# Rows of scores across four blocks in place of a carried state, in the gated linear recurrence of a hybrid block

## The chip, the cores and the metric

The kernel runs on one core of a Trainium2 chip. The metric is the device time of one execution in microseconds (us); of several runs the median counts, and lower is better. The core's engines work side by side, each through its own queue of instructions in order: TensorE (PE in the profile, with its weight loads as PEld), VectorE (DVE), ScalarE (ACT), GpSimd (POOL) and SyncE (SP), which issues most of the transfers (DMA).

## The reference, cut to what matters

One layer over 512 tokens of width 2048, all in float32. The input is normalised and projected; one branch is a gated linear recurrence (HGRN2) with 8 heads of 128 channels, the other a sparse attention in which an indexer scores all keys and the 128 best per query are kept. Both are gated, projected, merged, projected again and normalised. The recurrence is the part that changes most:

```python
def step(state, inp):            # one chunk of CHUNK = 64 tokens
    q_c, k_c, g_c, v_c = inp
    cum = jnp.cumsum(g_c, axis=1)                    # log of the decay
    inter = jnp.einsum('bthk,bhkv->bthv', q_c * jnp.exp(cum), state)
    diff = cum[:, :, None] - cum[:, None, :]
    decay = jnp.exp(jnp.where(causal[None, :, :, None, None], diff, -jnp.inf))
    scores = jnp.einsum('bthk,bshk,btshk->bhts', q_c, k_c, decay)
    intra = jnp.einsum('bhts,bshv->bthv', scores, v_c)
    last = cum[:, -1]
    new_state = (jnp.exp(last)[..., None] * state
                 + jnp.einsum('bshk,bshv->bhkv', k_c * jnp.exp(last[:, None] - cum), v_c))
    return new_state, inter + intra
...
top_val, top_idx = lax.top_k(score, topk)            # topk = 128, in the sparse branch
```

The chunk is only a way to compute it: the result is a causal sum over all earlier tokens, each with the product of the decays between the two tokens. So any grouping of the tokens gives the same output.

## The kernel before

The whole program is one list of jobs, and a job is a stretch of matmuls (projections of the normalised input, with weights that are loaded, split and multiplied chunk by chunk). The order is written out by hand: instructions are issued to each engine's queue in the order in which the Python code meets them. A large projection is done in three products of rounded parts (`mm3`, lines 75 to 77): `wh` is the rounded weight, `wl` what the rounding left, both made by `split` (line 71 on ScalarE, line 72 on VectorE) from the loaded `wr`. `prep(i, ahead)` issues the loads and splits of the chunks up to three ahead. `mm` (line 80) is a plain matmul.

Everything else runs in lanes: Python generators, each of which issues a small piece of work and yields. `pump()` is called every 24 matmuls or so of a job and lets each lane issue one piece: first the recurrence (`hgrn`), then the selection (`top`), then the attention (`att`), then norms and tables. So a piece of a lane stands in TensorE's queue between two runs of projection matmuls, and its results are needed when the next pump comes to the next piece.

The recurrence, `hgrn_gen(p)`, handles two heads at a time, in the order p = 3, 2, 0, 1, one pair after the other. Head `c` of a pair has four blocks of 128 tokens. Inside a block the scores are built in levels: level `l` multiplies queries of the second half of each group of 2^l tokens with keys of the first half (`scores`, small matmuls into `hl`), after which `decay(l)` (line 779, VectorE) multiplies those queries and keys with the running products `tot`. After level 7 a query carries the decay from its block's start, a key the decay to its block's end, and `S` holds the transposed score matrices inside the eight blocks of the pair (zeros are written by `G.memset` at level 4). Then come three pieces:

- the keys of the first three blocks are transposed on TensorE (`hkt`, line 852) and copied to `kd` (line 853, ScalarE);
- the states are built: `hp` holds keys times values for three blocks, line 865 copies the first into `st`, and line 867 adds the others with their decay, one after the other, on VectorE;
- the output `ho`: for each block the scores `S` times the values, and for all but the first the state `st` times the queries. ScalarE copies `ho` out, with its squares, and a norm and a gate follow.

All of these matmuls have plain float32 operands. The projections have operands of a rounded float32 type (fp32r in the profile's rows for the engines that write them).

The selection, `top_gen`, finds the 128 largest scores of each row in 16 rounds of MAX and MATCH_REPLACE on VectorE (lines 639 and 640), for widths of 256, 384 and 512 columns. It has a budget: at every pump it gets 2.7 less `R.load`, and a lane that puts much work on VectorE sets `R.load` high, so that fewer rounds are issued there.

At the start, `start()` reads the input in 16 parts, multiplies the first weights straight away (`pf`, line 80) and sums the squares of the input for the norm: `square(k)` on ScalarE, `add(k)` on VectorE (line 321). Five groups of parts are handled, and the squares of a group are taken one group later.

Of the kernel before, what the change touches and what calls it, by code (L numbers as in the profile page):

```python
# [50 lines left out]
def hybrid_block(ctx, tc, x, w_in, w_uq, w_qidx, w_ukv, w_pa, w_pb, w_out, rel_bias, final_norm_w,  # L51
# [207 lines left out]
    def start():  # L259
        R.v0 = enter("v0")  # L260
        R.x = enter("sums")
        p0 = enter("p0", side="right")
        R.xt = []
        for k in range(8):
            if k in (EVEN, EVEN + 1):
                R.x.tile([128, STILL if k == EVEN else 64 - STILL], F32, name=f"gap{k}")
            R.xt.append(R.x.tile([128, 2, T], F32, name=f"xt{k}", tag=f"sh{k}"))
            if k < 6:
                xs_l.append(R.x.tile([128, 4, 256], FR, name=f"sl{k}", tag=f"sl{k}"))
            else:  # L270
                R.dg = R.x.tile([128, 1024], F32, name=f"dg{k}", tag=f"sl{k}")
                if k == 6:
                    R.row, R.total = R.dg[:, 0:T], R.dg[:, T:]
        R.rinv = cols[:, 25:29]
        ident = R.dg[:, 0:128]
        parts = ((0, 2), (2, 4), (4, 8), (8, 12), (12, 16))
        wh, wl, wr = [], [], []
        sums = p0.tile([128, 2, T], F32, name="sums")

        def load_x(k, i=None):  # L280
            n = slice(0, 2) if i is None else slice(i, i + 1)
            SP.dma_start(R.xt[k][:, n, :], x_t[:, 2 * k + n.start:2 * k + n.stop, :])

        def load_w(c):
            k0, k1 = parts[c]
            wr.append(p0.tile([128, 4, 272], F32, name="fr", bufs=3))
            SP.dma_start(wr[c][:, 0:k1 - k0, :], w_first[:, k0:k1, :])

        A.dma_start(wc, w_norm)
        load_x(0, 0)  # L290
        load_w(0)
        load_x(0, 1)
        load_w(1)
        load_x(1)
        A.dma_start(ident, c_ident)
        A.dma_start(cols[:, 0:25], w_cols)

        def load_group(c):
            load_x(2 * c - 2)
            load_w(c)  # L300
            load_x(2 * c - 1)

        load_group(2)
        heat_src = p0.tile([128, 128], F32, name="rows")
        G.memset(heat_src, 1.0)
        G.tensor_copy(ones_r, heat_src)
        A.activation(R.rinv[:, 0:1], eps, AF.Sqrt)
        warm = mmp.tile([128, T], F32, name="acc")
        for _ in range(8):
            PE.matmul(warm[:, 0:128], ones, ones, start=True, stop=True)  # L310
        pools4 = [(mmp, "acc"), (sdp, "sd")] * 2
        accs = [pool.tile([128, T], F32, name="pf", tag=tag)[:, 0:272] for pool, tag in pools4]
        squares = {}

        def square(k):
            squares[k] = p0.tile([128, 2, T], F32, name="sq", bufs=3)
            A.activation(squares[k], R.xt[k], AF.Square)

        def add(k):
            if k:  # L320
                V.tensor_tensor(sums, squares.pop(0) if k == 1 else sums, squares.pop(k), op=OP.add)

        def three(c, n):
            k0, k1 = parts[c]
            xp, wp = ((xh, wh), (xl, wh), (xh, wl))[n]
            for k in range(k0, k1):
                for t in range(4):
                    mm(accs[t], xp[k // 4][:, k % 4, t * 128:t * 128 + 128], wp[c][:, k - k0, :],
                       k + n == 0, k == NK - 1 and n == 2)

        behind = ()
        for c, (k0, k1) in enumerate(parts):
            n = slice(0, k1 - k0)
            wh.append(p0.tile([128, 4, 272], FR, name="fh", bufs=3))
            wl.append(p0.tile([128, 4, 272], FR, name="fl", bufs=3))
            G.tensor_copy(wh[c][:, n], wr[c][:, n])
            for k in range(k0, k1):
                src = R.xt[k // 2][:, k % 2, :]
                hi, lo = xh[k // 4][:, k % 4, :], xl[k // 4][:, k % 4, :]
                A.activation(hi, src, AF.Copy, scale=wc[:, k:k + 1])  # L340
                V.scalar_tensor_tensor(lo, src, wc[:, k:k + 1], hi.bitcast(F32), op0=OP.mult, op1=OP.subtract)  # L341
            V.tensor_tensor(wl[c][:, n], wr[c][:, n], wh[c][:, n].bitcast(F32), op=OP.subtract)
            if c < 2:
                load_group(c + 3)
            if c == 2:
                load_ahead()
            if c == 4:
                prep(0, 1)
            pairs = range(k0 // 2, k1 // 2)
            for k in behind:  # L350
                square(k)
                add(k)
            behind = pairs
            for n in range(3):
                three(c, n)
        prep(0, 2)
        for k in behind:
            square(k)
            add(k)
        V.tensor_tensor(R.total, sums[:, 0, :], sums[:, 1, :], op=OP.add)  # L360
        R.first = accs
        leave("p0")
# [373 lines left out]
    def hgrn_gen(p):  # L736
        f, q = (hg[p, n] for n in "fq")
        gate = R.h.tile([128, 2, T], F32, name="hg")
        SP.dma_start(gate, gate_d[2 * p:2 * p + 2].rearrange("f p t -> p f t"))
        S = R.h.tile([128, 8, 128], F32, name="hS")  # L740
        near = R.h.tile([128, 8, 32], F32, name="hnear")
        G.memset(near, 0.0)
        qk = R.h.tile([128, 2, 2, T], F32, name="hqk")
# [60 lines left out]
        def spread_out(l, ps):  # L804
            m = 1 << (l - 1)
            for h in range(0, 128, 2 * m):
                for e in range(2):
                    g = h + m * e
                    A.activation(S[h:h + m, e::2, h + m:h + 2 * m],
                                 ps[g:g + m, 0:4 * m].rearrange("p (n t) -> p n t", n=4), AF.Copy)  # L810

        def nears(hs):
            for h in hs:
                A.activation(S[h:h + 32, :, h:h + 32], near[h:h + 32], AF.Copy)

        for l in range(1, 8):
            R.load = (0, 2.9, 1.6, 2.2, 1.5, 2.1, 1.4, 1.4)[l]
            if l % 2 == 0:
                do_soon()
                tot = decay(l)  # L820
                if l == 4:
                    G.memset(S, 0.0)
                if l == 6:
                    nears((0, 32))
                yield
                continue
# [18 lines left out]
        R.load = 0.0  # L845
        if p == 1:
            yield
        kd = R.h.tile([128, 2, 3, 128], F32, name="hkd")
        for c in range(2):
            pt = bank("hkt")  # L850
            for j in range(3):
                PE.transpose(pt[:, j * 128:(j + 1) * 128], k[:, c, j * 128:(j + 1) * 128], R.ident)
            A.activation(kd[:, c], pt[:, :384].rearrange("p (j t) -> p j t", j=3), AF.Copy)
        yield
        while (p, "v") not in hg:
            yield
        R.load = 1.4
        v = hg[p, "v"]
        st = R.h.tile([128, 2, 3, 128], F32, name="hst")
        for c in range(2):  # L860
            pp = bank("hp")
            for j in range(3):
                mm(pp[:, j * 128:(j + 1) * 128], kd[:, c, j, :], v[:, j, c * 128:(c + 1) * 128],
                   j == 0, True)
            A.activation(st[:, c, 0, :], pp[:, 0:128], AF.Copy)
            for j in (1, 2):
                V.scalar_tensor_tensor(st[:, c, j, :], st[:, c, j - 1, :],
                                       tot[:, c * 4 + j:c * 4 + j + 1],
                                       pp[:, j * 128:(j + 1) * 128], op0=OP.mult, op1=OP.add)
        yield  # L870
        sq = k
        zs = []
        o = place(p, [128, 2, T], F32, "ho", "hf")
        for c in range(2):
            po = bank("ho")
            for j in range(4):
                sl = slice(j * 128, (j + 1) * 128)
                mm(po[:, sl], v[:, j, c * 128:(c + 1) * 128], S[:, 4 * c + j, :], j == 0, j == 0)
                if j:
                    mm(po[:, sl], st[:, c, j - 1, :], q[:, c, sl], False, True)  # L880
            A.activation(o[:, c], po, AF.Copy, scale=128 ** -0.5)
            A.activation(sq[:, c], po, AF.Square, scale=128 ** -0.5)
        R.load = 0.0
        yield
        for c in range(2):
            zs.append((place(p, [128, T], FR, "hzh", ("hkd", "hst")[c]),
                       place(p, [128, T], FR, "hzl", ("hq", "hS")[c])))
            split(*zs[c], sq[:, c])
        R.load = 1.4
        yield  # L890
# [14 lines left out]
        V.tensor_tensor(sq, sq, o, op=OP.mult)  # L905
        yield
        R.load = 1.3
        for c in range(2):
            y = [place(p, [128, T], FR, f"hy{i}", (("hkd", "hst"), ("hq", "hS"))[i][c]) for i in range(2)]
            split(*y, sq[:, c])  # L910
            for i in range(2):
                late[1].append(lambda y=y[i], i=i, h=2 * p + c: SP.dma_start(ya_d[i, h], y.bitcast(F32)))
# [713 lines left out]
```

## Time and profile before

| what | value |
|---|---|
| median of 3 runs | 1341.34 us (1340.42 to 1341.58) |
| the profiled execution | 1340.78 us, of which the profile's span is 1339.0 us |
| TensorE busy | 1328.2 us, 99% of the span |
| VectorE busy | 1067.2 us, 80% |
| ScalarE busy | 667.4 us, 50% |
| GpSimd busy | 35.7 us, 3% |
| mean DMA rate | 154 GB/s |
| granted TensorE clock | 0.999 of full speed |

A row of a timeline has the start in us from the span's start, the busy us, engine, line, operation, the tiles written and read, and in brackets how long the engine was idle before and what released it. In the chain of waits a row has the start, the length and the piece of work, and consecutive instructions of one kind are one row with their count. A plain float32 matmul with two float32 operands stands in the trace as two records (two passes), so a count of x12 is six matmuls; a transpose has one.

### The profile page before, as it was taken

The page shows a single profiled execution, that of the slowest core. Times are in us where ns is not written, and L with a number is a line of the kernel's source. Part 1 is how long each engine was busy: PE and PEld are TensorE (multiplying, and loading weights), DVE is VectorE, ACT ScalarE, POOL GpSimd, SP SyncE. Part 2 cuts the span into 40 slices and gives each one's busy share as a digit, 9 for nine tenths or more (in the row PEclk, how much of TensorE's full clock was granted, in tenths as well). Part 3 has the DMA queues.
Part 4 walks back from the last instruction along what each step waited for, and adds up shares of the span by engine and source line. Part 5 has one row for each costly group of instructions (what it writes and reads, how often), then busy time and mean ns, then how long its engine had stood idle before and what let it go on. Part 6 is the DMA issues. An engine that isn't in the chain of part 4 may idle for free.

```text
span 1339.0 us, 26559 instructions
## 1 busy us (share of the span) xinstructions
PE 1328.2 (99%) x10876; PEld 1236.8 (92%) x10876; DVE 1067.2 (80%) x1705; ACT 667.4 (50%) x1060; POOL 35.7 (3%) x54
## 2 busy tenths in 40 slices
PE   9999999999999999999999999999999999999997
PEld 9988999999999999999999888888888888899996
DVE  7777889998888888886879989775656658899856
ACT  6455555454454444444666464656434423444435
POOL 2000000000000000000000000020001000000000
PEclk9999999999999999999999999999999999999999
DMA  6344545543454444434523525445755556653564
GB/s 242 95 114 113 151 142 158 154 138 104 142 158 143 142 142 142 135 107 164 182 84 103 182 72 159 125 151 176 242 191 191 186 177 218 202 161 124 163 208 164
DMA packets 141290, 205.82 MB, mean 154 GB/s; under 512 B 8672, under 2 KB 82032, under 8 KB 141040
## 3 DMA queue, kind: packets, MB, share of 16 engines
q1 hardware_dynamic: 140592, 203.78, 48.3%
q8 instruction: 85, 1.39, 0.4%
q10 hardware_dynamic: 576, 0.35, 0.1%
q14 instruction: 37, 0.30, 0.1%
HBM read 168.42 MB, written 35.68 MB: 152 GB/s over the span
## 4 chain that ended last, share of the span: by engine, by line
PE 95%; DVE 2%; ACT 1%; DMA 1%; issue 0%; SPq 0%; DVEq 0%; ACTq 0%
PE pp L75 15%; PE pp L77 15%; PE pp L76 15%; PE acc L75 14%; PE acc L77 14%; PE acc L76 14%; PE hl L80 1%; PE ho L80 1%; DMA xt<-in_x_t_dram 1%; PE sc L75 1%; PE sc L76 1%; PE sc L77 1%; PE hp L80 0%; PE po L77 0%; DVE xl L341 0%; PE po L76 0%
## 5 line engine op out<-in xcount | busy, mean ns | idle before, releaser
L150 ACT ACTIVATE bh<-wr 128x768 fp32r<-128x768 f32 x128 | 108.2, 845 | 215.5 <-issue 94.5
L152 ACT ACTIVATE wh<-sv 128x512 fp32r<-128x512 f32 x256 | 152.5, 623 | 84.3 <-DVE sv L145 66.6
L77 PE MATMUL pp<-sh,wl 128*128 128x256 f32 x624 | 172.7, 277 | 0.0
L75 PE MATMUL pp<-sh,wh 128*128 128x256 f32 x624 | 172.7, 277 | 0.0
L76 PE MATMUL pp<-sl,wh 128*128 128x256 f32 x624 | 172.6, 277 | 0.0
L72 DVE TENSOR_TENSOR wl<-wr,wh 128x1024 fp32r<-128x1024 f32 (+1 forms) x104 | 125.5, 1207 | 57.0 <-ACT wh L71 57.0
L154 DVE TENSOR_TENSOR wl<-sv,wh 128x1024 fp32r<-128x1024 f32 x128 | 156.4, 1222 | 5.8
L153 DVE TENSOR_TENSOR bl<-wr,bh 128x768 fp32r<-128x768 f32 x128 | 122.2, 955 | 47.2 <-ACT bh L150 46.9
L71 ACT ACTIVATE wh<-wr 128x1024 fp32r<-128x1024 f32 (+1 forms) x104 | 108.2, 1040 | 94.3 <-PE acc L76 40.6
L75 PE MATMUL acc<-xh,wh 128*128 128x512 f32 x304 | 120.3, 396 | 0.0
L77 PE MATMUL acc<-xh,wl 128*128 128x512 f32 x304 | 118.6, 390 | 0.0
L76 PE MATMUL acc<-xl,wh 128*128 128x512 f32 x304 | 118.5, 390 | 0.0
L76 PEld LDWEIGHTS pp<-sl,wh 128*128 128x128 f32 x624 | 117.3, 188 | 0.0
L77 PEld LDWEIGHTS pp<-sh,wl 128*128 128x128 f32 x624 | 117.3, 188 | 0.0
L75 PEld LDWEIGHTS pp<-sh,wh 128*128 128x128 f32 x624 | 117.3, 188 | 0.0
L75 PE MATMUL pp<-xh,bh 128*128 128x256 f32 x416 | 114.8, 276 | 0.0
L77 PE MATMUL pp<-xh,bl 128*128 128x256 f32 x416 | 114.8, 276 | 0.0
L76 PE MATMUL pp<-xl,bh 128*128 128x256 f32 x416 | 114.8, 276 | 0.0
L75 PE MATMUL acc<-yh,wh 128*128 128x512 f32 x256 | 100.3, 392 | 0.0
L76 PE MATMUL acc<-yl,wh 128*128 128x512 f32 x256 | 99.7, 390 | 0.0
L77 PE MATMUL acc<-yh,wl 128*128 128x512 f32 x256 | 99.7, 389 | 0.0
L145 DVE TENSOR_TENSOR sv<-wr 128x512 f32<-128x512 f32 x128 | 87.8, 686 | 8.2 <-DMA wr<-in_w_in_dram 5.1
(390 smaller groups left out, 3605.2 us busy)
## 6 DMA issues: line engine op xcount, KB each, us to landing
wr<-in_w_in_dram SPq DMA_DIRECT2D x136, 512.0 KB, 3.8
wr<-in_w_out_dram SPq DMA_DIRECT2D x32, 512.0 KB, 3.8
mg<-gate_d SPq DMA_DIRECT2D x48, 256.0 KB, 4.4
gate_d<-c SPq DMA_DIRECT2D x44, 256.0 KB, 4.7
wr<-in_w_in_dram SPq DMA_DIRECT2D x36, 256.0 KB, 3.0
wr<-in_w_pa_dram SPq DMA_DIRECT2D x16, 512.0 KB, 4.6
wr<-in_w_pb_dram SPq DMA_DIRECT2D x16, 512.0 KB, 4.1
wr<-in_w_qidx_dram SPq DMA_DIRECT2D x8, 512.0 KB, 4.0
```

The lines of the kernel that those rows point to most:

```text
L71: A.activation(hi, src, AF.Copy)
L72: V.tensor_tensor(lo, src, hi.bitcast(F32), op=OP.subtract)
L75: PE.matmul(ps, lh, rh, start=first, stop=False, skip_group_check=True)
L76: PE.matmul(ps, lh, rl, start=False, stop=False, skip_group_check=True)
L77: PE.matmul(ps, ll, rh, start=False, stop=last, skip_group_check=True)
L80: PE.matmul(ps, l, r, start=first, stop=last, skip_group_check=True)
L145: V.tensor_tensor(sv[:, 0:2, :], b[:, 1:3, :], b[:, 0:1, :].to_broadcast([128, 2, 256]), op=OP.add)
L150: A.activation(bh, b[:, 1:4, :], AF.Copy)
L152: A.activation(vh[:, i:i + 2, :], sv[:, i:i + 2, :], AF.Copy)
L153: V.tensor_tensor(bl, b[:, 1:4, :], bh.bitcast(F32), op=OP.subtract)
L154: V.tensor_tensor(vl, sv, vh.bitcast(F32), op=OP.subtract)
```

## The change

Three edits.

**The recurrence has no state any more.** `S` grows from 8 to 20 blocks of 128 columns: for each head the ten score blocks of the causal triangle (query block at or after the key block). They are laid out with changing steps, and `blocks` builds the access patterns. The transposes, `kd`, the `hp` matmuls, `st` and line 867 are gone. In their place stand two pieces: four matmuls of 128 columns (neighbouring blocks: key block 0 with query block 1, and 2 with 3, for both heads) with one copy of 512 columns, then one multiplication on VectorE (line 868) that carries the decay on for the queries of block 3 and the keys of block 0; and, one pump later, four matmuls of 256 columns (key blocks 0 and 1 with query blocks 2 and 3) with two copies of 512. The output is then four matmuls for each head, one for each key block, over 512, 384, 256 and 128 columns, with the values as weights. The number of pieces and of yields stays as it was. The zeros cover the diagonal blocks as before. Tiles that reused the places of `hkd` and `hst` (`hz`, `hy`) now reuse the place of `S`.

**The sums of squares at the start.** For the last group of parts (`c == 4`) the two additions of the group before it are issued after `prep(0, 2)`, behind the split of the second weight chunk, where they stood ahead of it.

**The selection.** While pair p = 3 is at levels 5 and 6, `R.load` is 1.2 higher.

```diff
--- before.py
+++ after.py
@@ -349,11 +349,16 @@
             pairs = range(k0 // 2, k1 // 2)
             for k in behind:
                 square(k)
+            for k in behind if c < 4 else ():
                 add(k)
+            if c == 4:
+                last = behind
             behind = pairs
             for n in range(3):
                 three(c, n)
         prep(0, 2)
+        for k in last:
+            add(k)
         for k in behind:
             square(k)
             add(k)
@@ -737,7 +742,11 @@
         f, q = (hg[p, n] for n in "fq")
         gate = R.h.tile([128, 2, T], F32, name="hg")
         SP.dma_start(gate, gate_d[2 * p:2 * p + 2].rearrange("f p t -> p f t"))
-        S = R.h.tile([128, 8, 128], F32, name="hS")
+        S = R.h.tile([128, 20, 128], F32, name="hS")
+
+        def blocks(at, dims, s=S):
+            return bass.AP(tensor=s.tensor, offset=s.offset + at * 128, ap=[s.ap[0], *dims])
+
         near = R.h.tile([128, 8, 32], F32, name="hnear")
         G.memset(near, 0.0)
         qk = R.h.tile([128, 2, 2, T], F32, name="hqk")
@@ -806,20 +815,21 @@
             for h in range(0, 128, 2 * m):
                 for e in range(2):
                     g = h + m * e
-                    A.activation(S[h:h + m, e::2, h + m:h + 2 * m],
-                                 ps[g:g + m, 0:4 * m].rearrange("p (n t) -> p n t", n=4), AF.Copy)
+                    o = blocks(3 - e, [[1280, 2], [-256, 2], [1, m]], S[h:h + m, :, h + m:h + 2 * m])
+                    A.activation(o, ps[g:g + m, 0:4 * m].rearrange("p (c i t) -> p c i t", c=2, i=2), AF.Copy)
 
         def nears(hs):
             for h in hs:
-                A.activation(S[h:h + 32, :, h:h + 32], near[h:h + 32], AF.Copy)
+                o = blocks(3, [[1280, 2], [-128, 4], [1, 32]], S[h:h + 32, :, h:h + 32])
+                A.activation(o, near[h:h + 32].rearrange("p (c j) t -> p c j t", c=2), AF.Copy)
 
         for l in range(1, 8):
-            R.load = (0, 2.9, 1.6, 2.2, 1.5, 2.1, 1.4, 1.4)[l]
+            R.load = (0, 2.9, 1.6, 2.2, 1.5, 2.1, 1.4, 1.4)[l] + (1.2 if p == 3 and l in (5, 6) else 0)
             if l % 2 == 0:
                 do_soon()
                 tot = decay(l)
                 if l == 4:
-                    G.memset(S, 0.0)
+                    G.memset(blocks(3, [[1280, 2], [-128, 4], [1, 128]]), 0.0)
                 if l == 6:
                     nears((0, 32))
                 yield
@@ -845,46 +855,46 @@
         R.load = 0.0
         if p == 1:
             yield
-        kd = R.h.tile([128, 2, 3, 128], F32, name="hkd")
+        ps = bank("h8")
         for c in range(2):
-            pt = bank("hkt")
-            for j in range(3):
-                PE.transpose(pt[:, j * 128:(j + 1) * 128], k[:, c, j * 128:(j + 1) * 128], R.ident)
-            A.activation(kd[:, c], pt[:, :384].rearrange("p (j t) -> p j t", j=3), AF.Copy)
+            for i in range(2):
+                s = slice(i * 256, i * 256 + 128)
+                mm(ps[:, (2 * c + i) * 128:(2 * c + i + 1) * 128], k[:, c, s],
+                   q[:, c, i * 256 + 128:i * 256 + 256], c == 0 and i == 0, True)
+        A.activation(blocks(5, [[1280, 2], [384, 2], [1, 128]]),
+                     ps.rearrange("p (c i t) -> p c i t", c=2, i=2), AF.Copy)
+        x = bass.AP(tensor=qf.tensor, offset=qf.offset + 384, ap=[qf.ap[0], [640, 2], [512, 2], [1, 128]])
+        tv = bass.AP(tensor=tot.tensor, offset=tot.offset + 2, ap=[tot.ap[0], [-1, 2], [4, 2], [0, 128]])
+        V.tensor_tensor(x, x, tv, op=OP.mult)
+        R.load = 0.7
+        yield
+        for c in range(2):
+            ps = bank("h9")
+            for i in range(2):
+                mm(ps[:, i * 256:i * 256 + 256], k[:, c, i * 128:i * 128 + 128], q[:, c, 256:512], i == 0, True)
+            A.activation(blocks(10 * c + 7, [[-384, 2], [256, 2], [1, 128]]),
+                         ps.rearrange("p (i n t) -> p i n t", i=2, n=2), AF.Copy)
+        R.load = 0.0
         yield
         while (p, "v") not in hg:
             yield
-        R.load = 1.4
         v = hg[p, "v"]
-        st = R.h.tile([128, 2, 3, 128], F32, name="hst")
-        for c in range(2):
-            pp = bank("hp")
-            for j in range(3):
-                mm(pp[:, j * 128:(j + 1) * 128], kd[:, c, j, :], v[:, j, c * 128:(c + 1) * 128],
-                   j == 0, True)
-            A.activation(st[:, c, 0, :], pp[:, 0:128], AF.Copy)
-            for j in (1, 2):
-                V.scalar_tensor_tensor(st[:, c, j, :], st[:, c, j - 1, :],
-                                       tot[:, c * 4 + j:c * 4 + j + 1],
-                                       pp[:, j * 128:(j + 1) * 128], op0=OP.mult, op1=OP.add)
-        yield
         sq = k
         zs = []
         o = place(p, [128, 2, T], F32, "ho", "hf")
         for c in range(2):
             po = bank("ho")
             for j in range(4):
-                sl = slice(j * 128, (j + 1) * 128)
-                mm(po[:, sl], v[:, j, c * 128:(c + 1) * 128], S[:, 4 * c + j, :], j == 0, j == 0)
-                if j:
-                    mm(po[:, sl], st[:, c, j - 1, :], q[:, c, sl], False, True)
+                n = (4, 3, 2, 1)[j]
+                mm(po[:, j * 128:], v[:, j, c * 128:(c + 1) * 128],
+                   blocks(10 * c + 3 - j, [[(256, 256, 896, 128)[j], n], [1, 128]]), j == 0, j == 3)
             A.activation(o[:, c], po, AF.Copy, scale=128 ** -0.5)
             A.activation(sq[:, c], po, AF.Square, scale=128 ** -0.5)
         R.load = 0.0
         yield
+        z = place(p, [128, 3, T], FR, "hzs", "hS")
+        zs = [(z[:, 0], place(p, [128, T], FR, "hzl", "hq")), (z[:, 1], z[:, 2])]
         for c in range(2):
-            zs.append((place(p, [128, T], FR, "hzh", ("hkd", "hst")[c]),
-                       place(p, [128, T], FR, "hzl", ("hq", "hS")[c])))
             split(*zs[c], sq[:, c])
         R.load = 1.4
         yield
@@ -905,8 +915,9 @@
         V.tensor_tensor(sq, sq, o, op=OP.mult)
         yield
         R.load = 1.3
+        ys = place(p, [128, 3, T], FR, "hys", "hS")
         for c in range(2):
-            y = [place(p, [128, T], FR, f"hy{i}", (("hkd", "hst"), ("hq", "hS"))[i][c]) for i in range(2)]
+            y = [ys[:, c], place(p, [128, T], FR, "hyl", "hq") if c == 0 else ys[:, 2]]
             split(*y, sq[:, c])
             for i in range(2):
                 late[1].append(lambda y=y[i], i=i, h=2 * p + c: SP.dma_start(ya_d[i, h], y.bitcast(F32)))
```

On TensorE the first place is the pair p = 3, where the piece with the states is replaced; `h_8936` and `h_8940` are the two banks for the scores of key blocks 0 and 1 with query blocks 2 and 3.

```order
 L76 MATMUL acc<-wl,xh_92 128x256
 L77 MATMUL acc<-wh,xl_95 128x256
-L80 MATMUL hp<-hv,hkd 128x128 x6
+L80 MATMUL h_8936<-hqk 128x256 x2
+L80 MATMUL h_8940<-hqk 128x256 x2
 L75 MATMUL acc<-wh,xh_93 128x256
 L76 MATMUL acc<-wl,xh_93 128x256
```

Six matmuls of 128 columns have become four of 256, between the same projection matmuls. One piece later on the same engine stands the output; of the program now:

```order
L77 MATMUL acc<-wh,xl_96 128x256
L80 MATMUL ho<-hS,hv 128x512
L80 MATMUL ho<-hS,hv 128x384
L80 MATMUL ho<-hS,hv 128x256
L80 MATMUL ho<-hS,hv 128x128
L80 MATMUL ho<-hS,hv 128x512
L80 MATMUL ho<-hS,hv 128x384
L80 MATMUL ho<-hS,hv 128x256
L80 MATMUL ho<-hS,hv 128x128
```

Before, 14 matmuls of 128 columns stood here (8 with `hS` and 6 with `hst`); now there are 8 over 2,560 columns in all.

On VectorE, pair p = 3 at level 6 (`hqk` with 16x32 is that level's `decay`), before:

```order
L792 COPY_PREDICATED hnear<-levels,hl 128x8x16
L639 MAX m_8754<-M 128x8
L640 MATCH_REPLACE M<-m_8754,M 128x256
L72 TENSOR_TENSOR ckl<-nt,ckh 128x512
L72 TENSOR_TENSOR wl<-wr,wh 128x1024
L779 TENSOR_TENSOR hqk<-hqk,tot_8750 128x2x16x32
L781 TENSOR_TENSOR tot_8793<-tot_8750 128x16
```

and now (lines 788 and 790 are the old 779 and 781):

```order
L801 COPY_PREDICATED hnear<-levels,hl 128x8x16
L72 TENSOR_TENSOR ckl<-nt,ckh 128x512
L72 TENSOR_TENSOR wl<-wr,wh 128x1024
L788 TENSOR_TENSOR hqk<-hqk,tot_8750 128x2x16x32
L790 TENSOR_TENSOR tot_8790<-tot_8750 128x16
L564 SCALAR_TENSOR_TENSOR nt<-ckv,cols,rr 128x512
```

One round of the selection (MAX and MATCH_REPLACE) no longer stands ahead of the decay of level 6, and the next one is gone from behind it. A little later on VectorE, where the new multiplication of line 868 is issued, now:

```order
L72 TENSOR_TENSOR ckl<-nt,ckh 128x512
L72 TENSOR_TENSOR wl<-wr,wh 128x1024
L868 TENSOR_TENSOR hqk<-hqk,tot_8846 128x2x2x128
L644 MAX m_8906<-M 128x8
L645 MATCH_REPLACE M<-m_8906,M 128x256
L644 MAX m_8909<-M 128x8
```

Before, the split `wl` was followed by three rounds of the selection and then by the four instructions of line 867. The new multiplication stands directly behind `wl`, and one piece earlier in the program than line 867 did.

## The prediction

> **What bounds the kernel now.** I read the page first (busy shares and the chain of waits by engine), then TensorE's own waits, then the busy time by stretch around the recurrences, and last the timelines of the places that the change touches.
>
> ```profile
> PE 1328.2 (99%) x10876; PEld 1236.8 (92%) x10876; DVE 1067.2 (80%) x1705; ACT 667.4 (50%) x1060; POOL 35.7 (3%) x54
> PE 95%; DVE 2%; ACT 1%; DMA 1%; issue 0%; SPq 0%; DVEq 0%; ACTq 0%
> ```
>
> TensorE is busy for 99% of the span and holds 95% of the chain that ended last. Busy time alone could hide a slow pace, so its waits come next (columns: us in total, times, longest).
>
> ```profile
> PE acc L310 <- POOL ones_r L306: 1.4, 1, 1.4
> PE hl L80 <- DVE hqk L779: 0.7, 1, 0.7
> PE pf L80 <- POOL fh L336: 0.3, 1, 0.3
> PE pf L80 <- ACT xh L340: 0.3, 1, 0.3
> ```
>
> Three of the four lie in the first ten us. The only one in the recurrences is the 0.7 us for a decay (line 779). The busy time by stretch, over the four pairs of heads:
>
> ```profile
> 690.00:720.00 30.00, 29.34 (x638) 28.29 (x637) 26.64 (x55) 17.44 (x28) 0.00 (x0) 1.00 0.33 100
> 720.00:780.00 60.00, 60.00 (x784) 53.54 (x784) 54.17 (x114) 32.90 (x50) 1.27 (x2) 1.00 0.48 146
> 780.00:840.00 60.00, 60.00 (x699) 49.98 (x699) 52.13 (x97) 33.67 (x50) 1.58 (x3) 1.00 0.40 120
> 840.00:900.00 60.00, 60.00 (x713) 50.66 (x712) 43.10 (x76) 34.67 (x58) 6.76 (x9) 1.00 0.45 137
> ```
>
> The first figure behind the length is TensorE: from 720 to 900 us it has no gap at all, at a granted clock of 1.00. So in this stage every instruction added to TensorE is paid in full, and work taken from VectorE or ScalarE is worth nothing unless TensorE waits for it. The question is what the new matmuls cost.
>
> **TensorE, the main term.** The old pieces of pair p = 3 in the chain of waits, with two rows from the start of the kernel that have other widths:
>
> ```profile
> 721.17 0.66 PE hkt L852 x6
> 724.56 1.34 PE hp L80 x12
> 728.73 3.12 PE ho L80 x28
> 731.85 0.47 PE t L80 x2
> 39.60 0.79 PE st L367 x8
> 43.22 0.86 PE st L380 x2
> ```
>
> The forms of those at line 80, 367 and 380 are
>
> ```profile
> L80 PE MATMUL ho<-hS,hv 128*128 128x128 f32 x64 | 11.0, 275 | 0.0
> L80 PE MATMUL t<-bf,flip 128*128 128x512 f32 x8 | 2.8, 431 | 0.0
> L367 PE MATMUL st<-ones_r,dg x8: 164/250/250, 39.4 to 40.1; 128*128 128x1 f32 x8
> L380 PE MATMUL st<-dg,ones_r x2: 590/590/591, 43.1 to 43.5; 128*128 128x512 f32 x2
> ```
>
> The lengths in the chain are what counts (a single duration of 275 or 590 ns overlaps its neighbours). Removed for each pair: 0.66 + 1.34 + 3.12 = 5.12 us, 46 passes of 128 columns at 0.111 us each.
>
> What does a wider float32 pass cost? The one such instruction is line 380: one plain float32 matmul of 512 columns, two passes, 0.86 us, so 0.43 us a pass. That is 3.9 times the 0.111 of 128 columns for 4 times the columns: the time goes with the columns, and merging saves some 4%. By that row:
>
> - neighbouring blocks: 4 matmuls of 128 columns, 8 passes x 0.111 = 0.89 us;
> - blocks 0 and 1 with 2 and 3: 4 matmuls of 256 columns, 8 passes x 0.215 = 1.72 us;
> - output: for each of 2 heads 2 passes each of 512, 384, 256 and 128 columns, 4 x (0.43 + 0.323 + 0.215 + 0.111) = 4.32 us.
>
> The sum is 6.93 us, against 5.12: 1.8 us more for each pair, **7.2 us for four**. In units of 128 columns it is 64 passes against 46; fewer instructions (16 against 26) with more columns. The bounds: all 64 at 0.111 give 7.10, so +2.0 a pair and +8.0 in all; all 64 at a quarter of 0.43 give 6.88, so +1.76 a pair and +7.0 in all. I take 7.2, since line 380 is the same kind of instruction.
>
> The Trainium skill speaks here through two pages. TensorE: Matmul & The Clock Gate, Back-to-back issue gap, gives the time between matmuls as columns / 2.4 + 2.5 ns, 216 ns for 512; the two 512-column matmuls of `t`, in the rounded type, bear it out (0.47 / 2 = 0.235 us), line 380 does not. FP8 and Floating Point Precision, TensorE Precision Notes, says that a true float32 matmul takes four passes; line 380 agrees (0.86 us is four times 0.215), though the trace lists them as two records. By the first rule alone the new matmuls would be cheap, which is the rival below.
>
> **VectorE and ScalarE in p = 3.** Here lies the one wait in the recurrences, and the edit of the selection aims at it.
>
> ```profile
> 713.59 0.42 DVE L639 MAX8 m<-M 128x8 f32<-128x256 f32 x1
> 714.45 0.68 DVE L72 TENSOR_TENSOR ckl<-nt,ckh 128x512 fp32r<-128x512 f32 x1
> 716.19 1.22 DVE L779 TENSOR_TENSOR hqk<-hqk,tot 128x1024 f32<-128x1024 f32 x1
> 717.46 0.69 PE L80 MATMUL hl<-hqk 128*64 128x64 f32 x16 [0.66 <-DVE hqk L779]
> 722.59 1.06 ACT L71 ACTIVATE wh<-wr 128x1024 fp32r<-128x1024 f32 x1
> 723.69 1.23 DVE L72 TENSOR_TENSOR wl<-wr,wh 128x1024 fp32r<-128x1024 f32 x1 [1.03 <-ACT wh L71]
> 724.40 1.50 PE L80 MATMUL hp<-hv,hkd 128*128 128x128 f32 x12
> L72 DVE TENSOR_TENSOR hzl<-hqk,hzh 128x512 fp32r<-128x512 f32 x8 | 5.2, 687 | 7.4 <-ACT hzh L71 7.4
> ```
>
> The round of the selection from 713.59 to 714.45 is held back, so the decay of level 6 ends 0.86 us earlier, and TensorE's wait of 0.66 us goes: −0.7. But the new multiplication of line 868 (512 columns, priced by the row of `hzl` at 0.65 us from start to start) is needed by the very first of the 256-column matmuls, one piece earlier in the program than line 867 was needed, and on VectorE it stands behind the split `wl`, which waits for `wh` on ScalarE. ScalarE is itself late there with its copies into `hS`, which start when the scores of level 7 end. With all of it 0.66 us earlier, `wl` runs from 723.03 to 724.2 and line 868 to 724.85. TensorE would be there at 724.40 − 0.66 + (0.89 − 0.66) = 723.97. So it waits 0.9 us at a place where it did not wait before: +0.9. Behind it on TensorE stand all projections; nothing there is late in its turn. Net of both: **+0.2 us**. Bounds: −0.7 (line 868 is in time after all) and +0.9 (the old wait stays as well).
>
> **The other three pairs.** The tightest is the third:
>
> ```profile
> 838.92 1.06 ACT L71 ACTIVATE wh<-wr 128x1024 fp32r<-128x1024 f32 x1
> 840.01 1.23 DVE L72 TENSOR_TENSOR wl<-wr,wh 128x1024 fp32r<-128x1024 f32 x1 [1.17 <-ACT wh L71]
> 842.28 1.50 PE L80 MATMUL hp<-hv,hkd 128*128 128x128 f32 x12
> L639 DVE MAX8 m<-M 128x8 f32<-128x512 f32 x16 | 11.0, 688 | 0.1
> ```
>
> Line 868 would run there from 841.16 to 841.8, 0.7 us before 842.28 + 0.23. No wait; if the next round of the selection came ahead of it (0.69 us for its MAX and about as much for its MATCH_REPLACE), it would cost 0.7. The order of instructions puts that round behind line 868 in all four pairs. Line 867, which goes, and `kd` and `st` on ScalarE were covered by TensorE's projections, and so are the three new copies of 512 columns: at 0.6 us each (the row of `ho`), 1.8 us against 1.54 (two of 0.49 and two of 0.28, `hkd` and `hst`; all three rows below), with the next need 2.7 us later. Zero, for both.
>
> ```profile
> L853 ACT ACTIVATE hkd<-hkt x8: 486/492/502, 723.5 to 897.0; 128x384 f32<-128x384 f32 x8
> L865 ACT ACTIVATE hst<-hp x8: 277/278/279, 725.3 to 901.0; 128x128 f32<-128x128 f32 x8
> L881 ACT ACTIVATE ho<-ho x8: 597/598/601, 730.3 to 908.0; 128x512 f32<-128x512 f32 x8
> ```
>
> **The start.** The additions move behind the second split.
>
> ```profile
> 28.84 2.28 PE L80 MATMUL pf<-fl,xh 128*128 128x272 f32 x16
> 29.84 2.55 DVE L321 TENSOR_TENSOR sums<-sums,sq 128x1024 f32<-128x1024 f32 x2
> 32.30 1.22 DVE L72 TENSOR_TENSOR wl<-wr,wh 128x1024 fp32r<-128x1024 f32 x1
> 36.61 0.28 PE L75 MATMUL acc<-wh,xh 128*128 128x256 f32 x1
> 36.02 0.69 DVE L360 TENSOR_TENSOR dg<-sums 128x512 f32<-128x512 f32 x1
> ```
>
> The last early wait, for the low part at 28.84, is behind nothing that moves. The second split ends near 31.0 in place of 33.5, but its chunk is needed only at 36.61, by the 49th product of the first projection. The sum `dg` still ends near 36.7, for the matmuls of line 367 at 39.4. The next weights load 2.4 us earlier: no wait of TensorE for a load exists to be shortened. Zero; if the sums came 3 us later it would begin to cost.
>
> **The sum.** 7.2 + 0.2 = 7.4 us on the profiled execution's 1340.78 us (its span 1339.0 and 1.8 around it) is 1348.2; the median of the runs is 0.56 above that execution, so **1348.7 us**. Own range: the lower ends (7.0 − 0.7) and the upper ones (8.0 + 0.9) give 1347.6 to 1350.2, with 0.6 on each side for the runs 1347.0 to 1350.8.
>
> **The rivals.**
>
> *Wide rows at one column per cycle (faster).* If a float32 pass of many columns ran at the pace of the rounded type, `t`'s 0.235 us for 512, the new work would be 0.89 + 8 x 0.1175 + 4 x (0.235 + 0.176 + 0.1175 + 0.111) = 4.4 us a pair, 0.7 less than 5.12: −2.9 in all, 1338.5. For it: the pass with a single column (line 367) takes 0.79 / 8 = 0.099 us, nearly as long as one with 128, so short passes have a floor that wide ones would not pay, and there are 32 passes for 46. It decides if the pass of 512 columns takes less than 0.29 us (0.89 + 0.44 + 13 times that pass would be 5.12). Against: line 380 has 0.43.
>
> *More waits (slower still).* Line 868 sits between two pieces with one round of projections between them. If in the other three pairs it stood behind one late `wl` as in p = 3, up to 0.9 us for each would be added: 1348.7 + 2.7 = 1351.4. For it: ScalarE has the longer copies ahead of `wh`. Against: the margins above.
>
> *The extra passes are hidden (no change).* It would need TensorE to have 7 us of gaps in 690 to 925 us; it has 0.7. 1341 to 1342.
>
> **Chances.** Forecast 0.78, more waits 0.12, wide rows 0.06, hidden 0.04. Between 1338.7 and 1344.0 (0.2% on each side, about what a measurement can tell) counts as the same; the wide-row rival falls on that edge, so half of it each way: faster 0.03, same 0.07, slower 0.90. The range of 8 in 10 takes the forecast's own and most of the second rival: 1346.2 to 1351.5.
>
> **What would show it.** The pieces in the chain of waits: some 0.9, 1.7 and 4.3 us in place of 0.66, 1.34 and 3.12 for each pair. TensorE's wait for `hqk` at level 6 gone, and one of about 0.9 us for the new line 868 near 724 us. No other new wait, the end of the span the same. The forecast is wrong if `ho` takes less than 3.1 us, or if TensorE shows waits for line 868 in more than one pair.

## The result and the profile after

The changed kernel takes 1349.39 us (median of 4 runs, 1349.18 to 1349.96) against 1340.92 us for the kernel before (4 runs, 1340.42 to 1341.58): 8.5 us more. The ratio is 1.0061 with a 95% interval of 1.0049 to 1.0074, so it is slower, by 0.6%. The profiled execution took 1349.18 us with a span of 1347.3 us, 8.4 us more than that of before. In a later session one run of the kernel before (3337.15 us) and one of the kernel with one more yield (1373.52 us at a granted clock of 0.948) lie far from the others of their kernels, and the medians below leave these two out.

The page of the changed kernel, busy shares and the chain of waits by engine:

```profile
PE 1336.3 (99%) x10820; PEld 1237.5 (92%) x10820; DVE 1067.1 (79%) x1693; ACT 668.5 (50%) x1056; POOL 41.2 (3%) x54
PE 93%; DVE 3%; DMA 2%; ACT 1%; issue 1%; SPq 0%; DVEq 0%; ACTq 0%
```

TensorE is busy for 8.1 us more than before, with 56 records fewer; VectorE is where it was, ScalarE is busy for 1.1 us more and GpSimd for 5.5 us more. The chain of waits has the new pieces of the recurrence, here pairs p = 3, 2 and 0 (columns: start, length, line and count; of p = 3 the first piece, with the same 8 passes, lies outside the chain):

```profile
725.28 1.99 PE h L80 x8
730.02 4.31 PE ho L80 x16
783.81 0.89 PE h L80 x8
787.46 1.73 PE h L80 x8
791.94 4.32 PE ho L80 x16
843.60 0.89 PE h L80 x8
847.24 1.73 PE h L80 x8
851.73 4.31 PE ho L80 x16
```

They take 0.89 + 1.73 + 4.31 = 6.93 us where 5.12 stood. In p = 3 the second piece starts behind a wait, and its row is 1.99 us long. TensorE's waits now (us in total, times, longest):

```profile
PE acc L310 <- POOL ones_r L306: 1.4, 1, 1.4
PE h L80 <- DVE hqk L868: 0.8, 1, 0.8
PE pf L80 <- ACT xh L340: 0.4, 2, 0.2
```

The wait for the decay of level 6 is gone and one for line 868 is there. How it comes about is in the timelines of ScalarE, VectorE and TensorE in p = 3:

```profile
722.30 1.06 ACT L71 ACTIVATE wh<-wr 128x1024 fp32r<-128x1024 f32 x1
723.39 1.23 DVE L72 TENSOR_TENSOR wl<-wr,wh 128x1024 fp32r<-128x1024 f32 x1 [1.37 <-ACT wh L71]
724.53 0.69 DVE L868 TENSOR_TENSOR hqk<-hqk,tot 128x512 f32<-128x512 f32 x1
724.23 0.28 PE L77 MATMUL acc<-wh,xl 128*128 128x256 f32 x1
725.28 1.99 PE L80 MATMUL h<-hqk 128*128 128x256 f32 x8 [0.77 <-DVE hqk L868]
```

Line 868 stands behind `wl`, `wl` behind `wh`, and TensorE, which was done with the projection matmuls ahead, stands idle for 0.77 us. The cost there is larger than this idle time: by the starts in the timeline, `h` begins 1.05 us after the last projection matmul (724.23 and 725.28), where such matmuls follow one another after 0.12 us.

Where the 8.3 us of span come from is best seen in the time from the first burst of score matmuls of one pair to that of the next. In the chain of waits of the kernel before these are

```profile
694.85 1.21 PE hl L80 x84
755.60 1.21 PE hl L80 x84
814.46 1.21 PE hl L80 x84
866.99 1.21 PE hl L80 x84
```

and after

```profile
695.28 1.21 PE hl L80 x84
758.28 1.21 PE hl L80 x84
819.01 1.21 PE hl L80 x84
873.41 1.21 PE hl L80 x84
```

| stretch | before | after | more |
|---|---|---|---|
| up to pair p = 3 | 694.85 | 695.28 | 0.4 |
| pair p = 3 to 2 | 60.75 | 63.00 | 2.25 |
| pair 2 to 0 | 58.86 | 60.73 | 1.87 |
| pair 0 to 1 | 52.53 | 54.40 | 1.87 |
| pair 1 to the end of the span | 472.0 | 473.9 | 1.9 |

Four pairs at 1.87 are 7.5 us of the 8.3, of which the matmuls themselves are 4 x 1.81 = 7.2.

### The profile page after: what moved, and what is told of

Read it like the earlier page. It is cut to its first block, busy times and chain, and to the rows that moved or that the text cites. A ratio compares the mean times of both kernels' runs of the same rounds, so it can differ in the third digit from the quotient of the medians.

```text
span 1347.3 us, 26430 instructions
## 1 busy us (share of the span) xinstructions
PE 1336.3 (99%) x10820; PEld 1237.5 (92%) x10820; DVE 1067.1 (79%) x1693; ACT 668.5 (50%) x1056; POOL 41.2 (3%) x54
## 3 DMA queue, kind: packets, MB, share of 16 engines
q8 instruction: 85, 1.39, 0.4%
## 4 chain that ended last, share of the span: by engine, by line
PE 93%; DVE 3%; DMA 2%; ACT 1%; issue 1%; SPq 0%; DVEq 0%; ACTq 0%
PE pp L75 15%; PE pp L77 15%; PE pp L76 15%; PE acc L75 13%; PE acc L77 13%; PE acc L76 13%; PE hl L80 1%; PE ho L80 1%; DMA xt<-in_x_t_dram 1%; PE h L80 1%; DMA wr<-in_w_out_dram 1%; PE sc L75 1%; PE sc L76 1%; PE sc L77 1%; DVE o L1488 1%
```

## The experiments

The theory at this point: float32 matmuls are paid by their columns (1), TensorE has no slack in this stage (2), the held selection saves one wait and the new multiplication brings another (3), and the start does nothing (4). The rivals: that the cost is in the number of instructions, that part of the work was hidden, that the two waits are one and the same, that holding the selection or the order at the start costs something elsewhere.

**Wide matmuls cut into pieces of 128 columns.**

```diff
-                mm(ps[:, i * 256:i * 256 + 256], k[:, c, i * 128:i * 128 + 128], q[:, c, 256:512], i == 0, True)
+                for u in range(2):
+                    mm(ps[:, i * 256 + u * 128:i * 256 + u * 128 + 128], k[:, c, i * 128:i * 128 + 128],
+                       q[:, c, 256 + u * 128:384 + u * 128], i == 0 and u == 0, True)
...
-                mm(po[:, j * 128:], v[:, j, c * 128:(c + 1) * 128], ...)
+                for u in range(n):
+                    mm(po[:, (j + u) * 128:(j + u + 1) * 128], v[:, j, c * 128:(c + 1) * 128], ...)
```

> The changed kernel with its wide float32 matmuls cut into pieces of 128 columns: the same columns, 24 instructions of 128 in place of 4 of 256 and 8 of 512 to 128 (per pair 64 passes in all). If the time goes with the columns (my theory): the two pieces of work take 16 x 0.111 = 1.78 and 40 x 0.111 = 4.45 us per pair in place of 1.73 and 4.31, so +0.2 us per pair and about +0.8 us in all, near 1350.2. If a pass had a floor that wide rows escape (rival: it is the instructions that cost), 64 passes in place of 32 would add clearly more, at the 0.099 us of a one-column pass up to 3 us per pair, 1361.

Measured: 1352.29 us against 1341.36 for the kernel before in the same session, 10.9 us more (ratio 1.0079, 1.0063 to 1.0095). Its chain of waits, pair p = 2, and TensorE's longest wait:

```profile
784.65 0.89 PE h L80 x8
788.29 1.78 PE h L80 x16
792.84 4.46 PE ho L80 x40
PE acc L77 <- issue: 1.8, 1, 1.8
```

The pieces take 1.78 and 4.46 us, within 0.01 us of what was expected of 16 and 40 passes of 128 columns, and 0.20 us more than the wide ones. So from 128 columns up the columns decide; 56 passes in place of 24 add 3%. The total, 10.9 us over the kernel before, is 1.6 us above the 9.3 expected (8.5 and 0.8). The profiled execution has a wait of 1.8 us between projection matmuls, away from the pieces (below). Whether the pieces bring it about isn't shown: with them TensorE's program is longer, 86 packets in place of 85. Whether all four runs (1351.16 to 1352.37) had it isn't known.

**Without the scores between the two halves.**

```diff
-            for i in range(2):
-                mm(ps[:, i * 256:i * 256 + 256], k[:, c, i * 128:i * 128 + 128], q[:, c, 256:512], i == 0, True)
-            A.activation(blocks(10 * c + 7, [[-384, 2], [256, 2], [1, 128]]), ...)
...
-                n = (4, 3, 2, 1)[j]
-                mm(po[:, j * 128:], v[:, j, c * 128:(c + 1) * 128],
+                n = (2, 1, 2, 1)[j]
+                mm(po[:, j * 128:(j + n) * 128], v[:, j, c * 128:(c + 1) * 128],
```

> The changed kernel without the scores between the two halves of the sequence: the four matmuls of 256 columns and their copies are left out, and the output uses only the blocks on and next to the diagonal inside each half (six blocks for each head in place of ten), so a query does not see keys of the other half. My theory (TensorE pays each column in full, nothing is hidden): per pair 1.73 us less for the scores and 4.31 - 2.61 = 1.70 us less for the output, 3.4 us, and no wait for the decay of line 868 (0.8 us): 13.7 + 0.8 = 14.5 us less, near 1334.9. If part of the extra matmuls had been hidden behind other waits, less than that comes back: at half, 1342.

Measured: 1334.12 us (1333.37 to 1335.55), 7.2 us less than the kernel before in the same session (ratio 0.9947, 0.9930 to 0.9965), where 14.5 less than 1349.4, so 6.0 less than the kernel before, had been expected. Its chain of waits shows the output and the bursts that give the length of a pair:

```profile
785.42 2.62 PE ho L80 x16
694.74 1.21 PE hl L80 x84
752.95 1.22 PE hl L80 x84
810.76 1.21 PE hl L80 x84
861.70 1.21 PE hl L80 x84
```

From pair 0 to pair 1 it is 50.94 us in place of 54.40, 3.46 less, for 1.73 + 4.31 − 2.62 = 3.42 us of matmuls left out. Behind pair 1 it is 3.5 us less, and from pair 2 to 0, where this execution has a wait of 0.40 us that names nothing, 2.9. From pair 3 to 2 it is 58.21 in place of 63.00, 4.8 less: 3.4 for the matmuls, and 1.4 for the wait for line 868, which is gone with them and had been put at 0.8. So what is taken off TensorE comes back whole: nothing was hidden.

**The changed kernel without the held selection.**

```diff
-            R.load = (0, 2.9, 1.6, 2.2, 1.5, 2.1, 1.4, 1.4)[l] + (1.2 if p == 3 and l in (5, 6) else 0)
+            R.load = (0, 2.9, 1.6, 2.2, 1.5, 2.1, 1.4, 1.4)[l]
```

> The changed kernel without the higher load in the selection for pair p = 3. My theory: the wait of 0.66 us for the decay of level 6 is back, and the wait for line 868 stays at about 0.9 us since ScalarE's copies start later by as much as TensorE does: +0.7 us, near 1350.1. Rival: the two waits are one and the same lateness of VectorE, so that with the first wait back the second shrinks, and the total stays at 1349.4.

Measured: 1349.78 us (1349.45 to 1350.29), 8.4 us over the kernel before of the same session (ratio 1.0062). TensorE's waits:

```profile
PE h L80 <- DVE hqk L868: 0.8, 1, 0.8
PE hl L80 <- DVE hqk L788: 0.7, 1, 0.7
```

Both waits stand side by side, so they are not one lateness shared out. From pair 3 to pair 2 it takes 63.40 us (bursts at 695.68 and 759.08) where the changed kernel takes 63.00 in its first profile and 62.78 in its second (bursts at 694.29 and 757.07): the hold is worth 0.4 or 0.6 us there, where 0.7 had been expected; in the totals it can't be told.

**One more yield between line 868 and the matmuls that need it, in p = 3.**

```diff
         R.load = 0.7
         yield
+        if p == 3:
+            yield
```

> The changed kernel with one more yield in pair p = 3 between the multiplication of line 868 and the matmuls that need it, so 24 projection matmuls (2.8 us) stand between. My theory: the wait of 0.77 us is gone and nothing else becomes late: -0.8 us, near 1348.6. Rival: ScalarE's copies then come behind the next split and the output waits instead: 1349.4 or more.

Measured: 1350.75 us (three runs, 1349.94 to 1351.14), 9.4 us over the kernel before of the same session (ratio 1.0068, 1.0050 to 1.0086). The wait for line 868 is gone, as expected, but three others are there:

```profile
PE hl L80 <- DVE hqk L755: 1.1, 1, 1.1
PE hl L80 <- issue: 0.8, 1, 0.8
PE hl L80 <- DVE hqk L788: 0.6, 1, 0.6
```

The rival had the outcome right and the place wrong. Everything behind p = 3 in the lane comes one pump later, and the waits for lines 755 and 788 are at the start of pair p = 1, near 874 and 882 us, where VectorE has other work ahead of the new pair's first product and decay. The third is a wait for nothing that the profile names. So in this execution the shift by one pump brings waits of 1.7 us for VectorE and removes one of 0.8. The totals fit that (9.4 us over the kernel before, where the changed kernel has 8.5), but their intervals overlap.

**The held selection alone, in the kernel before.**

```diff
-            R.load = (0, 2.9, 1.6, 2.2, 1.5, 2.1, 1.4, 1.4)[l]
+            R.load = (0, 2.9, 1.6, 2.2, 1.5, 2.1, 1.4, 1.4)[l] + (1.2 if p == 3 and l in (5, 6) else 0)
```

> The kernel before with the higher load in the selection alone. My theory: TensorE's one wait in the recurrences (0.7 us for the decay of level 6 in p = 3) goes and nothing comes in its place, since the state is needed a piece later than the multiplication of line 868: -0.7 us, near 1340.3. Rival: the held selection comes back later as a wait for the mask or the attention: 0 or more.

Measured: 1340.94 us (11 runs, 1339.60 to 1341.80) against 1340.88 (21 runs): a ratio of 1.0000, 0.9991 to 1.0008. No gain shows in the runs, but this interval is 1.1 us wide on each side, so a gain of 0.7 us is not excluded either. In the trace of one execution the wait for line 779 is gone, and this one is new, in the burst of level 5 (timeline of TensorE):

```profile
710.41 0.57 PE L80 MATMUL hl<-hqk 128*32 128x16 f32 x46
711.75 0.32 PE L80 MATMUL hl<-hqk 128*32 128x16 f32 x16 [0.78 <-issue]
```

To see whether the hold brings it, the same kernel was profiled twice more, with a second profile of each of the two original kernels beside it.

> The kernel before with the held selection, looked at a second time. The first look had no wait for line 779 but one of 0.78 us for nothing that the profile names, inside the burst of small matmuls near 711 us, where a 16 KB packet of the instruction queue started 1.8 us later than in the kernel before. If that wait is chance (my theory: a packet of instructions came late), this look has no gap there, or one at another burst; if the held selection causes it, the gap of about 0.8 us is at the same burst again.

> The kernel before with the held selection, a third look. Chance: no gap near 711 us, or one at another burst. Caused by the held selection: the gap of about 0.8 us at the same burst again.

> The kernel before, a second look. If waits for instructions are chance, it may have one of 0.4 to 1.8 us in a burst of small matmuls too; the wait of 0.66 us for line 779 near 717 us is there again in any case.

> The changed kernel, a second look. The pieces of the recurrence take 0.89, 1.73 and 4.31 us again and the wait for line 868 about 0.77 us. From the first product at 39 us to the first score of the indexer the first look took 0.4 us longer than the kernel before; by my theory that is chance, and this look is nearer to 597.1 us.

In both new profiles of the held selection TensorE waits for nothing behind the start; from pair 3 to pair 2 it takes 59.73 us (bursts at 696.20 and 755.93, and at 695.04 and 754.77), against 60.45 in the second profile of the kernel before (695.68 and 756.13), where the wait for line 779 stands again. So in the traces the hold is worth 0.7 us, as predicted, where the wait without a name stays away. That wait doesn't come with the hold each time; whether the hold makes it likelier is open (below). The second profile of the changed kernel repeats the pieces:

```profile
724.07 1.99 PE h L80 x8
728.81 4.31 PE ho L80 x16
PE h L80 <- DVE hqk L868: 0.8, 1, 0.8
```

That execution took 1347.88 us beside 1341.3 for the kernel before, one run of each, 6.6 us more. Its stretch from pair 3 to 2, 62.78 us, also prices the wait for line 868: it is 3.05 us over the 59.73 of the hold alone, which has no wait there. Of this, 1.87 us are what another pair has more, so some 1.2 us remain for the wait. By the starts of instructions in the trace, from the first matmul of the statistics at 38.75 us to the first score of the indexer it took 597.23 us; the first profile had 597.46, the kernel before 597.09 and 597.07, two other executions 597.51 (one of the three with the hold) and 597.55 (the extra yield), and the rest, among them four more with the order of the changed kernel in that stretch, 597.04 to 597.11. So the 0.4 us up to pair 3 in the table above belong to that execution and not to the change.

**The order at the start alone, in the kernel before.**

```diff
             for k in behind:
                 square(k)
+            for k in behind if c < 4 else ():
                 add(k)
+            if c == 4:
+                last = behind
...
         prep(0, 2)
+        for k in last:
+            add(k)
```

> The kernel before with the order of the sums of squares at the start alone. My theory: nothing, 1340.9 within 0.4; the second split ends 2.4 us earlier and TensorE waits for it neither before nor after. Rival: the earlier load of the next weights shortens or lengthens a wait in the first 50 us: the first projection would start earlier or later by some 0.4 us.

Measured: 1340.68 us (11 runs, 1340.52 to 1343.25) against 1340.88: a ratio of 1.0000, 0.9991 to 1.0009. Nothing that these runs can tell, as expected.

## Why the prediction was right, step by step

Forecast 1348.7 us with 1346.2 to 1351.5, measured 1349.4.

*What bounds the kernel.* TensorE without slack from 690 to 925 us: right. Leaving matmuls out gave 3.46 us a pair for 3.42 us of matmuls.

*The cost of the new matmuls.* Forecast 0.89 + 1.72 + 4.32 = 6.93 us, measured 0.89 + 1.73 + 4.31 = 6.93. The one row of 512 float32 columns at line 380 was enough to price them, and the cut into pieces shows that neither bound would have been far off. What this sum left out is 0.06 us a pair, the difference between 1.87 for a whole stage and 1.81 for its pieces; where it lies isn't shown.

*Pair p = 3.* The old wait goes and a new one of 0.9 us comes for line 868 behind `wl`: right in place and mechanism, and TensorE's idle time there is 0.77. The net was given as +0.2; the table has 2.25 − 1.87 = +0.4. The old wait was priced well (0.7). The new one costs more than its idle time: some 1.2 us by the stretches of the hold alone and of the second profile of the changed kernel.

*The other pairs, and the start.* No wait in the other three: right. At the start the second split ends near 31.1 us and `dg` near 36.9, as forecast within 0.2, and TensorE doesn't wait for them: right.

*The sum.* +7.4 forecast, +8.5 by the medians and +8.4 by the two profiled executions. No step failed. The 1.0 us between the profiled executions and the forecast is 0.2 (four times 0.06), 0.2 in p = 3, 0.4 ahead of the recurrences, which belong to that execution, and 0.2 that is not placed. How near the total came is in part luck: single executions scatter by about a microsecond, and that of the second profile of the changed kernel came out at +6.6.

*The rivals.* Wide rows at one column per cycle: excluded by `ho` itself, 4.31 us for 2,560 columns, 1.68 ns each. The Trainium skill's page TensorE: Matmul & The Clock Gate, Back-to-back issue gap, has columns / 2.4 + 2.5 ns, by estimate 0.42 ns a column; the measurement decides against it for plain float32, while the rounded type is near it (`t`, 0.235 us for 512 columns, where the formula gives 0.216). The Trainium skill's page FP8 and Floating Point Precision, TensorE Precision Notes, has four passes for true float32, and 1.68 is four times 0.42: the trace agrees in time, though it lists two records. Hidden passes: excluded by the kernel without the far scores. More waits in the other pairs: not there, though the kernel with one more yield has two of them.

## What to carry to other kernels

On an engine without slack, count what the instructions stream, not how many they are, as long as they are wide (here from 128 columns up; the pass with one column in the prediction takes nearly as long as one with 128). Here 26 matmuls became 16 and cost 1.8 us more, because plain float32 columns went from 46 times 128 to 64 times 128. A carried state is what keeps a recurrence linear in its length; scores over whole rows give that up, and with the four blocks of this kernel that is already the dearer form, 64 passes against 46 (no run varies the number of blocks). A wait of less than a microsecond that is shifted by one place in a hand-written order came back somewhere else here, so such an edit should be judged by the length of its stage in several profiles, not by the total.

## What the runs showed of the hardware that was not expected

**TensorE seems to wait for its own instructions at times.** One DMA queue carries kind "instruction" and moves 85 packets in the kernel before:

```profile
q8 instruction: 85, 1.39, 0.4%
```

Its 1.39 MB are 64 bytes for each of TensorE's 10,876 matmuls and 10,876 weight loads (21,752 x 64 = 1.392 MB), so it seems to be TensorE's program. A burst of score matmuls takes 84 matmuls and as many loads in 1.2 us and so uses them up much faster than the projections, with one matmul in 0.11 to 0.23 us. The packet ahead of the burst of level 5 in p = 3, with its landing as the time since the first score matmul of that pair (worked out from the starts and lengths of packets and matmuls in the traces):

```
kernel                        landing, us after the first score matmul    wait in the burst of level 5, us
before, two profiles          13.4   13.7                                  none
order at the start alone      13.1                                         none
hold alone, three profiles    15.2   13.9   13.4                           0.78   none   none
changed, two profiles         13.5   13.5                                  none
changed, without the hold     13.8                                         none
changed, one more yield       14.9                                         0.78
changed, pieces of 128        13.4                                         none
without the far scores        13.1                                         none
```

The wait appears in the two executions, of twelve, in which the packet landed about a microsecond or more later than in the others, and TensorE went on 1.5 us after the landing (710.28 and 711.75, 709.84 and 711.33). The waits for "issue" of 1.8 us in the kernel with pieces of 128 and of 0.4 us in the one without the far scores have such a packet too: landed at 829.2 and 760.4, TensorE on at 830.5 and 761.75. This is a coincidence of times in twelve traces, not a cause that is shown: no run makes a packet late. Why the packet came late in some executions stays open too. Both waits in the burst of level 5 are in kernels with the held selection, two executions of the eight that have it; the four without it have none, which is too few to say that the hold plays no part.

**The start scatters.** The first matmul of the statistics comes between 38.75 and 40.71 us, two us apart in the twelve profiles, with no order by kernel: 39.44 and 40.29 for the kernel before, 39.49 and 38.75 for the changed one. With the instruction waits this is about the size of what separates single runs, and more than the two smaller edits of this change could show in these totals.
